# Gates and branch projections of a hybrid decoder layer as seven block products in two stages around attention

## The chip, the cores and the metric

One core of a Trainium2 chip runs the kernel. The metric is the device time of one execution in microseconds. Engines: TensorE (PE, matmuls; PEld is its weight load), VectorE (DVE), ScalarE (ACT), GpSimd (POOL), SyncE (SP, whose queue issues nearly all transfers).

## What is computed

One decoder layer over 1024 tokens of width 1024, float32. The reference, cut to what matters:

```
z = h @ w_in
hq, hf, hi, hg, sq, sk, sv, mq, gl = split_cols(z, IN_SPLITS)   # gl: 3 x 1024 gate columns
o_a = hgrn2(hq, hf, hi, lb)                    # 8 heads of 128, chunks of 64 tokens
o_a = rms_norm(o_a) * hg_norm_gain * silu(hg)
o_b = sliding_window_attention(sq, sk, sv, rel_bias, sinks)     # 16 heads, window 128
o_c = memory_attention(mq, mk, mv)             # 4 heads of 256, 256 memory tokens
gates = sigmoid(gl)
merged = (gates[0] * (o_a @ w_branch_hg) + gates[1] * (o_b @ w_branch_swa)
          + gates[2] * (o_c @ w_branch_mem))
h = layer_norm(alpha * h + merged @ w_out)
h = layer_norm(alpha * h + square(relu(h @ w_up)) @ w_down)
```

## The kernel before

**Products in three matmuls.** Every float32 operand is split in two parts: ACT casts it to the high part, DVE or POOL subtracts to get the low part (`split`, line 74). A product is then high times high, high times low and low times high. `zt` (line 99) makes 128 output columns for the 512 tokens of a half: 8 blocks of k, 24 matmuls of 512 columns. `weight` (line 78) loads 512 KB into a raw tile R, casts and subtracts into W; its subtraction goes to DVE every third time, else to POOL (line 70). There are four R and four W tiles, and the PSUM banks are three z, three s and two t.

**Stages.** First the keys and values of the memory tokens (lines 158 to 213). Then, for each half of the tokens (line 539): sliding-window attention (`swa_phase`), with gate blocks as matmul work between its units (`fill`); its eight branch projections (`proj`); memory attention by heads (`mem_head`); gates and projections in turn; HGRN2 (`hg_gates`, `hg_head`), where each head has a query product `z_q`, an output gate product `z_g`, a middle part `mid`, an output part `outp` and `last`; gates and projections again; then the product with w_out, LayerNorm and transposes (`flip_h1`, kept in `deferred`). Attention outputs stay on chip as split operands in O tiles; `merged` collects the gated sums. Weights of gates and projections are loaded and split once for each half.

**The up and down products** already use seven block products for two halves of the tokens and two halves of k (lines 700 to 952): of the eight products of half blocks one is saved, for sums and differences of the operands. `xs[1]` to `xs[7]` are the seven token operands, w1 to w4 the combined weights; a pair of weight blocks costs 7 x 12 = 84 matmuls. For the first 8 pairs (EARLY) two of the seven are made ahead by `first_two`.

**Order.** The code gives the tiles and a priority in program order; which instruction an engine takes next is then planned at build time by list scheduling on estimated durations, so that a weight of a later block may be cast before the result of an earlier one is read. Each engine and each queue then runs its list in order.

Of the kernel before, what the change touches and what calls it, by code (L numbers as in the profile page):

```python
# [15 lines left out]
P = 128  # L16
D = 1024
# [11 lines left out]
EARLY = 8  # L29

# [4 lines left out]
def hybrid_layer(ctx: ExitStack, tc: tile.TileContext, a: dict, out: bass.AP):  # L35
# [90 lines left out]
    bcon = st("MG", [P, 2048])[:32, :272]  # L126
# [3 lines left out]
    reset = const("reset", [P, 512])  # L130
    nc.vector.memset(reset, 1.0)
    nc.vector.memset(reset.rearrange("p (c t) -> p c t", t=64)[:, :, 0:1], 0.0)
    at = const("at", [P, 4, P])
    nc.gpsimd.memset(at, 0.0)
    state = const("state", [P, 8, P])
    carry = const("carry", [P, 3, P], F32R)
    vv = const("vv", [P, 5, P])
# [9 lines left out]
    d_h1t = dr.tile([P, NK, TH], F32, name="d_h1t")  # L147

    xsrc = a["xT"].rearrange("(k p) t -> p k t", p=P)
    msrc = a["memT"].rearrange("(k p) t -> p k t", p=P)  # L150
    mh = [st("T", [P, 4, MEM], F32R) for _ in range(2)]
    ml = [st("T", [P, 4, MEM], F32R) for _ in range(2)]
# [19 lines left out]
    x = (st("X", [P, NK, TH], F32R), st("X", [P, NK, TH], F32R))  # L172
    for h in range(4):
# [36 lines left out]
        if h < 3:  # L210
            load_x(xsrc[:, :, 0:TH], h, x, nc.vector)
            if h == 2:
                load_x(xsrc[:, :, 0:TH], 3, x, nc.vector)
# [13 lines left out]
    deferred = []  # L227

    def swa_unit(hf, tp, n, q, kk, bt, px, ob):
# [5 lines left out]
        def scores():  # L235
# [54 lines left out]
    def swa_phase(hf, x, merged, fill_last):  # L290
# [27 lines left out]
        def z_gate(m):  # L318
            o = zt(a["w_gate"][8 + m], *x)
            nc.scalar.activation(merged[m // 4][:, m % 4, :], o, AF.Tanh, scale=0.5)  # L320

# [7 lines left out]
        while deferred:  # L329
            deferred.pop(0)()  # L330
        oh = st("O", [P, NK, TH], F32R)
        ol = st("O", [P, NK, TH], F32R)
        pxa = st("T", [P, 2, 2, TH])
        pend = None
        for tp in range(4):
            if tp < 3:
                qn = st("T", [P, 2, 2, TH], F32R)
                fill = [lambda: z_sq(qn, tp + 1, 0), lambda: z_gate(2 * tp), lambda: z_sq(qn, tp + 1, 1),
                        lambda: z_gate(2 * tp + 1)]
            else:  # L340
                fill = [lambda: z_gate(6), lambda: z_gate(7)] + fill_last
            for n in range(4):
# [9 lines left out]
                def pend(pv=pv, n=n, tp=tp, ob=ob):  # L352
                    pv()
                    if n % 2:
                        cols = slice((n - 1) * P, (n + 1) * P)
                        src = ob.rearrange("p (n t q) -> p t n q", n=2, t=2)
                        for t in range(2):
                            evict_split(oh[:, 2 * tp + t, cols].rearrange("p (n q) -> p n q", n=2),
                                        ol[:, 2 * tp + t, cols].rearrange("p (n q) -> p n q", n=2), src[:, t])
            if tp < 3:  # L360
                q = qn
        pend()
        return oh, ol

    def gate(br, m, x):
        o = zt(a["w_gate"][8 * br + m], *x)
# [710 lines left out]
```

## Time and profile before

| | before |
|---|---|
| median of 3 runs | 2169.95 us (2169.92 to 2175.44) |
| the profiled execution | 2174.51 us, span 2171.3 us |
| PE busy, matmuls | 2096.4 us (97%), 10242 |
| DVE, ACT, POOL busy | 1141.3, 827.8, 844.8 us |
| HBM read, written | 216.78 MB, 44.58 MB |

Busy time of an engine counts the instructions that ran, also while they were held up; issue of transfers isn't counted. The span runs from the first to the last instruction of the profiled execution, whose own time is a little longer. What an engine's idle time costs is read from the stretch where it lies.

### The profile page before, as it was taken

To read this page: it belongs to the slowest core of one execution; us is meant where nothing else is said; L and a number is where in the kernel's file an instruction comes from. 1 tells how busy PE (TensorE), PEld (TensorE's weight loads), DVE (VectorE), ACT (ScalarE), POOL (GpSimd) and SP (SyncE) were. 2 spreads that over 40 slices of the span, in tenths; PEclk is the share of its full clock that TensorE was granted. 3 is DMA by queue.
4 is the path that set the end of the run, shared out by engine and by line. 5 is a ranking of instruction groups with operands and counts; after the bars stand their busy time and mean duration, and the time that the engine had idled before them with its cause. 6 is when DMAs were issued, how large, how long until landed. Compare 5 with 4: busy or idle time off the path is not lost.

```text
span 2171.3 us, 26697 instructions
## 1 busy us (share of the span) xinstructions
PE 2096.4 (97%) x10242; PEld 1725.8 (79%) x10242; DVE 1141.3 (53%) x2041; ACT 827.8 (38%) x1462; POOL 844.8 (39%) x401
## 2 busy tenths in 40 slices
PE   8999999999999999999999999996899998999987
PEld 8767888898988876678888898885788886888865
DVE  5566242244542366634315454137466565688888
ACT  5344242243433253424324343234444555433321
POOL 2212223423325441122343232554433435776675
PEclk9999999999999999999999999998899999999999
DMA  8411223222233541122332222344565446745322
GB/s 276 136 59 59 88 88 99 96 88 78 78 97 116 175 146 49 59 80 88 104 91 88 78 87 88 113 150 142 168 223 189 160 155 244 250 136 160 113 78 78
DMA packets 103422, 263.09 MB, mean 121 GB/s; under 512 B 9040, under 2 KB 22528, under 8 KB 103296
## 3 DMA queue, kind: packets, MB, share of 16 engines
q1 hardware_dynamic: 102400, 258.24, 36.7%
q10 hardware_dynamic: 896, 3.16, 0.4%
q8 instruction: 80, 1.31, 0.2%
q14 instruction: 46, 0.38, 0.1%
HBM read 216.78 MB, written 44.58 MB: 120 GB/s over the span
## 4 chain that ended last, share of the span: by engine, by line
PE 84%; DVE 5%; POOL 4%; issue 3%; DMA 2%; ACT 2%; SPq 0%; POOLq 0%; DVEq 0%; ACTq 0%
PE pz L60 59%; PE ps L60 17%; PE pt L60 7%; POOL W L76 1%; DMA R<-in_w_up_dram 1%; PE pt L274 1%; POOL sm L979 1%; DVE T L718 1%; ACT W L75 1%; POOL BT L76 0%; DVE R L718 0%; POOL O L994 0%; POOL MG L76 0%; DVE S L266 0%; DMA R<-d_ff 0%
## 5 line engine op out<-in xcount | busy, mean ns | idle before, releaser
L76 POOL TENSOR_TENSOR W<-R,W 128x1024 fp32r<-128x1024 f32 x200 | 485.9, 2430 | 1039.3 <-ACT W L75 1001.6
L60 PE MATMUL pz<-X,W 128*128 128x512 f32 x3360 | 821.8, 398 | 13.8 <-ACT W L75 10.1
L60 PEld LDWEIGHTS pz<-X,W 128*128 128x128 f32 x3360 | 628.5, 190 | 157.4 <-issue 11.5
L75 ACT CAST W<-R 128x1024 fp32r<-128x1024 f32 (+1 forms) x303 | 310.4, 1026 | 385.7 <-PE pz L60 156.0
L60 PE MATMUL pz<-O,W 128*128 128x512 f32 x1152 | 266.8, 390 | 0.0
L60 PEld LDWEIGHTS pz<-O,W 128*128 128x128 f32 x1152 | 215.8, 188 | 45.6 <-issue 0.8
L76 DVE TENSOR_TENSOR W<-R,W 128x1024 fp32r<-128x1024 f32 (+1 forms) x105 | 131.3, 1251 | 114.7 <-ACT W L75 114.3
L375 DVE SCALAR_TENSOR_TENSOR G<-G,pz 128x512 f32<-128x512 f32 x32 | 22.0, 687 | 174.1 <-PE pz L60 174.0
L60 PE MATMUL ps<-W,BT 128*128 128x512 f32 x360 | 98.9, 392 | 10.1 <-POOL BT L76 7.8
L60 PE MATMUL pz<-W,BT 128*128 128x512 f32 x354 | 97.4, 393 | 0.2 <-DVE X L880 0.2
L60 PE MATMUL pt<-O,W 128*128 128x512 f32 x384 | 93.9, 393 | 0.8 <-DVE T L718 0.8
L60 PE MATMUL pz<-W,X 128*128 128x256 f32 x768 | 93.7, 283 | 0.0
L60 PEld LDWEIGHTS pz<-W,X 128*128 128x128 f32 x768 | 92.9, 192 | 0.3
L76 POOL TENSOR_TENSOR BT<-R,BT 128x1024 fp32r<-128x1024 f32 x27 | 70.0, 2595 | 52.9 <-ACT BT L75 52.9
L60 PEld LDWEIGHTS ps<-W,BT 128*128 128x128 f32 x360 | 67.6, 188 | 25.8 <-POOL BT L76 8.2
L60 PEld LDWEIGHTS pt<-O,W 128*128 128x128 f32 x384 | 71.9, 189 | 18.5 <-DVE T L718 3.8
L76 POOL TENSOR_TENSOR MG<-R,MG 128x1024 fp32r<-128x1024 f32 (+1 forms) x30 | 78.9, 2632 | 16.5 <-ACT MG L75 16.5
L377 POOL TENSOR_TENSOR MG<-MG,G 128x512 f32<-128x512 f32 x32 | 42.3, 1321 | 99.7 <-DVE G L375 99.7
L60 PEld LDWEIGHTS pz<-W,BT 128*128 128x128 f32 x354 | 67.0, 190 | 15.4 <-DVE X L880 0.7
L60 PE MATMUL ps<-W,MG 128*128 128x512 f32 x252 | 68.2, 402 | 4.3 <-DVE O L880 4.3
L60 PE MATMUL ps<-W,T 128*128 128x256 f32 (+1 forms) x432 | 67.5, 294 | 0.0
L60 PE MATMUL pz<-W,MG 128*128 128x512 f32 x252 | 66.6, 396 | 0.0
(245 smaller groups left out, 3026.1 us busy)
## 6 DMA issues: line engine op xcount, KB each, us to landing
R<-d_ff SPq DMA_DIRECT2D x49, 512.0 KB, 3.6
R<-in_w_gate_dram SPq DMA_DIRECT2D x48, 512.0 KB, 3.5
R<-in_w_b_dram SPq DMA_DIRECT2D x48, 512.0 KB, 3.5
R<-in_w_up_dram SPq DMA_DIRECT2D x40, 512.0 KB, 4.2
d_ff<-T SPq DMA_DIRECT2D x58, 256.0 KB, 3.0
d_ff<-S SPq DMA_DIRECT2D x48, 256.0 KB, 2.5
T<-in_w_down_dram SPq DMA_DIRECT2D x12, 1024.0 KB, 5.5
R<-in_w_sq_dram SPq DMA_DIRECT2D x16, 512.0 KB, 3.6
```

The source lines that it names most:

```text
L60: nc.tensor.matmul(o, lhsT=l, rhs=r, start=start, stop=stop, skip_group_check=more)
L75: (hi_copy or nc.scalar.copy)(hi, src)
L76: (lo_eng or nc.gpsimd).tensor_tensor(out=lo, in0=src, in1=f32(hi), op=ALU.subtract)
L274: nc.tensor.transpose(o[:, c:c + P], pr[:, 2 * t + i, :], ident)
L375: nc.vector.scalar_tensor_tensor(out=t, in0=t, scalar=1.0, in1=o, op0=ALU.add, op1=ALU.mult)
L377: nc.gpsimd.tensor_tensor(out=mg, in0=mg, in1=th, op=ALU.add)
L718: nc.vector.tensor_tensor(out=o, in0=a_, in1=b_, op=op)
L979: nc.gpsimd.tensor_tensor(out=y, in0=e, in1=mhalf[:, :1], op=ALU.pow)
```

## The change

All gates (24 blocks of columns) and the HGRN2 output gate (8 blocks) are computed for both halves of the tokens in a stage of their own ahead of attention, as 16 pairs of blocks with seven products each; the results, after tanh (and for the output gate the product), go to DRAM (`d_z`). The left operand of x is split first, the other five are made from both halves (`combine`); four pairs make two of their products early (`two`). Attention then runs for both halves, one after the other. In it the forget gates `one` take the place of the gate blocks between the window units, `z_g` is gone (`zload` reads its result), the scalings of a unit's four rows are one instruction, and attention outputs are copied and stored in DRAM (`d_o`). During half 1 and the first projections, `job` loads the outputs of both halves, makes the combinations on POOL and stores them in `d_c`. A stage after attention then runs three branches in the order window, memory, HGRN2: seven operands loaded and split anew for each (`load_op`), two pairs early, four pairs of seven products, and `b_emit` multiplies by the gate loaded from `d_z` and adds to the merged sum, on POOL from the second branch on. Merged sums lie in `con`, T tiles and DRAM (`d_mg`) and are split by `merge_into`. Then the products with w_out run for both halves in a row, with half 0's transposes between half 1's blocks; the up stretch takes half 1's one at a time.

```diff
+    def combine(left, right, part, eng):
+        b11, b21, b12, b22 = left[0], left[1], right[0], right[1]
+        part(3, b22, 0)
+        eng.tensor_tensor(out=b11, in0=b12, in1=b11, op=ALU.subtract)
+        part(5, b11, 1)
...
+    def two(src, keep, emit):
+        w1 = halves(load_raw(src), nc.gpsimd)
+        o = pt("z")
+        prod(o, w1, 0, 1)
+        s1 = keep(o)
+        d = pt("s")
+        prod(d, w1, 1, 2)
+        emit(0, d, s1)
+
+    def seven(src0, src1, p1, emit):
+        r0 = load_raw(src0)
...
+        r1 = load_raw(src1)
+        add(r0[:, L], r0[:, L], r1[:, L], ALU.subtract)
+        add(r1[:, L], r1[:, L], r1[:, H])
+        w2 = halves(r1, nc.gpsimd)
+        add(r1[:, H], r1[:, H], r0[:, L], ALU.subtract)
+        w4 = st("W", [P, 2, 1024], F32R)
+        split(w4[:, 0, L], w4[:, 1, L], r1[:, H], nc.vector)
+        add(r0[:, H], r0[:, H], r1[:, H], ALU.subtract)
+        w3 = halves(r0, nc.gpsimd)
...
+        prod(o, w4, 0, 6, p1 is not None)
+        s2 = snap(o) if p1 is None else plus(o, p1)
+        b_ = pt("t")
+        prod(b_, w2, 0, 5)
+        prod(o, w3, 0, 7, False)
+        s3 = snap(o) if p1 is None else plus(o, p1)
+        emit(3, b_, s3)
+        c = pt("s")
+        prod(c, w2, 1, 4)
+        emit(1, c, s3)
+        prod(b_, w3, 1, 3, False)
+        emit(2, b_, s2)
...
+    for i in range(EARLY_Z):
+        two(zsrc(i)[0], z_keep(i), z_first(i))
+    for i in range(16):
+        seven(*zsrc(i), z_p1(i) if i < EARLY_Z else None, z_emit(i))
...
+    def job(br, k):
+        hs = (slice(0, TH), slice(TH, S))
+        t = []
+        for hv in hs:
+            raw = st("R", [P, 2, TH])
+            nc.sync.dma_start(raw, d_o[br, k:k + 5:4, :, hv].rearrange("k p t -> p k t"))
+            t.append((raw[:, 0], raw[:, 1]))
+
+        def part(j, src, e):
+            if j != 3:
+                nc.sync.dma_start(d_c[br, j - 4, k], src)
+
+        combine(t[0], t[1], part, nc.gpsimd)
...
-            for j in range(4):
-                nc.vector.tensor_scalar(out=pr[:, j, :], in0=pr[:, j, :], scalar1=dn[:, j:j + 1],
-                                        scalar2=None, op0=ALU.mult)
+            nc.vector.tensor_tensor(out=pr, in0=pr, in1=dn.unsqueeze(2).broadcast_to([P, 4, P]), op=ALU.mult)
...
+        for h in range(8):
...
+            if h < 7:
+                head(h + 1)
+            if h:
+                heads[h - 1][2]()
+            if h % 2 == 0 and h < 6:
+                g = h // 2 + 1
+                zv(vs[g // 2][:, g % 2], g)
+            heads[h][1]()
+            if h:
+                heads[h - 1][3]()
...
+            turn_b[0] += 1
+            split(xs[j][0][:, k:k + 2], xs[j][1][:, k:k + 2], raw, nc.gpsimd if turn_b[0] % 2 else nc.vector)
...
+        def emit(b, o, s_):
+            t = st("S", [P, 2, TH])
+            th, v = t[:, 0], t[:, 1]
+            nc.sync.dma_start(th, d_z[4 * br + i, b])
+            home = accs.get((i, b))
+            if home is None and e:
+                mg = st("G", [P, TH])
+                nc.sync.dma_start(mg, d_mg[slot[i, b]])
+            add(v, o, s_)
+            if e == 0:
+                dst = th if home is None else home
+                nc.vector.scalar_tensor_tensor(out=dst, in0=th, scalar=1.0, in1=v, op0=ALU.add, op1=ALU.mult)
+            else:
+                nc.vector.scalar_tensor_tensor(out=th, in0=th, scalar=1.0, in1=v, op0=ALU.add, op1=ALU.mult)
+                dst = th if home is None else home
+                nc.gpsimd.tensor_tensor(out=dst, in0=mg if home is None else home, in1=th, op=ALU.add)
...
+    for e in range(3):
+        br = order[e]
+        w = a[wname[br]]
+        for i in range(EARLY_B):
+            two(w[2 * i], lambda o, i=i: snap(o, p1s[i]), b_emit(e, i))
+            if i == 0:
+                operand_tiles()
+                load_op(br, 6)
+                load_op(br, 5)
+            else:
+                load_op(br, 7)
+                load_op(br, 4)
+                load_op(br, 3)
+        for i in range(4):
+            seven(w[2 * i], w[2 * i + 1], (lambda i=i: p1s[i]) if i < EARLY_B else None, b_emit(e, i))
+            if e == 0 and i in (1, 2):
+                job(0, i + 1)
+        if e < 2:
+            operand_left()
+            load_op(order[e + 1], 1)
+            load_op(order[e + 1], 2)
```

## Rows read from the trace of the kernel before

**Rows 1.** The page's first part: busy time, share of the span, instructions.

```profile
PE 2096.4 (97%) x10242; PEld 1725.8 (79%) x10242; DVE 1141.3 (53%) x2041; ACT 827.8 (38%) x1462; POOL 844.8 (39%) x401
```

**Rows 2.** The chain that ended last, shares of the span by engine.

```profile
PE 84%; DVE 5%; POOL 4%; issue 3%; DMA 2%; ACT 2%; SPq 0%; POOLq 0%; DVEq 0%; ACTq 0%
```

**Rows 3.** Busy time by stretch: length, engines (instructions), granted clock, DMA share, GB/s.

```profile
0.00:56.00 56.00, 49.27 (x387) 48.23 (x388) 30.92 (x43) 29.21 (x37) 12.74 (x10) 1.00 0.82 275
56.00:227.00 171.00, 167.16 (x805) 122.58 (x803) 105.60 (x366) 71.02 (x209) 34.24 (x16) 0.99 0.26 82
756.00:942.00 186.00, 175.70 (x850) 128.56 (x849) 124.03 (x389) 80.56 (x226) 48.70 (x26) 0.96 0.26 82
...
1700.00:1812.00 112.00, 112.00 (x494) 92.30 (x493) 62.51 (x75) 60.24 (x90) 43.23 (x18) 1.00 0.48 158
...
1850.00:2100.00 250.00, 249.73 (x1085) 203.59 (x1084) 201.76 (x216) 96.80 (x103) 180.38 (x69) 1.00 0.47 156
```

**Rows 4.** PE's instructions in order of time, projections and gates in turn (start, length).

```profile
342.71 5.60 PE L60 MATMUL pz<-O,W 128*128 128x512 f32 x24
348.15 5.60 PE L60 MATMUL pz<-X,W 128*128 128x512 f32 x24
```

**Rows 5.** The same view at the start of half 1; in brackets the idle time before.

```profile
776.04 1.11 PE L326 MATMUL pt<-cst,G 128*128 128x128 f32 x4 [3.84 <-ACT G L308]
776.80 8.11 PE L60 MATMUL pz<-X,W 128*128 128x512 f32 x24
784.76 1.04 PE L657 MATMUL pt<-cst,O 128*128 128x128 f32 x8
```

**Rows 6.** Groups by line and shape: busy us, mean ns of one, idle before.

```profile
L377 POOL TENSOR_TENSOR MG<-MG,G 128x512 f32<-128x512 f32 x32 | 42.3, 1321 | 99.7 <-DVE G L375 99.7
L76 DVE TENSOR_TENSOR W<-T,W 128x1024 fp32r<-128x1024 f32 x21 | 41.5, 1975 | 6.6 <-ACT W L75 6.5
...
L266 DVE TENSOR_SCALAR S<-S,sm 128x128 f32<-128x128 f32 x128 | 35.4, 340 | 0.6
...
L93 DVE TENSOR_TENSOR O<-ps,O 128x256 fp32r<-128x256 f32 x32 | 13.4, 419 | 11.6 <-ACT O L92 11.2
```

**Rows 7.** One line of the kernel: shortest, median and longest duration in ns.

```profile
L445 DVE TENSOR_SCALAR T<-T,c x16: 486/487/488, 419.7 to 1255.9; 128x512 f32<-128x512 f32 x16
```

**Rows 8.** Waits of PE: us in total, times, longest.

```profile
PE pt L274 <- DVE S L266: 10.1, 6, 1.9
```

**Rows 9.** One head: its stretch, then PE's and DVE's instructions in order.

```profile
607.67:622.95 15.28, 15.28 (x90) 13.27 (x88) 9.01 (x21) 5.99 (x15) 5.41 (x3) 1.00 0.22 70
...
614.12 0.83 PE L60 MATMUL ps<-BT 128*128 128x128 f32 x6
614.71 5.72 PE L60 MATMUL pz<-X,W 128*128 128x512 f32 x24
...
618.94 0.69 DVE L524 TENSOR_TENSOR BT<-ps,sm 128x512 f32<-128x512 f32 x1
```

**Rows 10.** POOL's and DVE's instructions in order of time, up and down products.

```profile
1706.22 2.41 POOL L76 TENSOR_TENSOR W<-R,W 128x1024 fp32r<-128x1024 f32 x1 [7.37 <-ACT W L75]
1708.94 2.51 POOL L76 TENSOR_TENSOR W<-R,W 128x1024 fp32r<-128x1024 f32 x1 [0.30 <-ACT W L75]
...
1707.38 1.81 DVE L718 TENSOR_TENSOR S<-T 128x512 f32<-128x512 f32 x1 [1.64 <-ACT T L727]
1709.11 0.68 DVE L718 TENSOR_TENSOR T<-ps,G 128x512 f32<-128x512 f32 x1
...
1711.92 0.68 DVE L718 TENSOR_TENSOR S<-T,S 128x512 f32<-128x512 f32 x1
...
1879.09 2.41 POOL L76 TENSOR_TENSOR BT<-R,BT 128x1024 fp32r<-128x1024 f32 x1 [2.68 <-ACT BT L75]
...
1880.34 2.23 DVE L76 TENSOR_TENSOR W<-T,W 128x1024 fp32r<-128x1024 f32 x1
```

**Rows 11.** The page's 40 slices: GB/s that the DMA engines moved.

```profile
GB/s 276 136 59 59 88 88 99 96 88 78 78 97 116 175 146 49 59 80 88 104 91 88 78 87 88 113 150 142 168 223 189 160 155 244 250 136 160 113 78 78
```

More of the change, by code (lines that the diff above doesn't have):

```diff
@@ L227, in hybrid_layer, with prod, snap @@
     deferred = []
+    L, H = slice(0, TH), slice(TH, 2 * TH)
+    def prod(o, w, g, j, start=True):
+        hi, lo = xs[j]
+        for k in range(4):
+            c = g * TH + k * P
+            wh, wl = w[:, 0, c:c + P], w[:, 1, c:c + P]
+            mm(o, wh, hi[:, k, :], start and k == 0, False, not start)
+            mm(o, wh, lo[:, k, :], False, False, not start)
+            mm(o, wl, hi[:, k, :], False, k == 3, not start)
+    def snap(o, t=None):
+        if t is None:
+            t = st("G", [P, TH])
+        nc.scalar.copy(t, o)
+        return t
@@ new lines, in add, with plus, load_raw, halves @@
+    def add(o, a_, b_, op=ALU.add):
+        nc.vector.tensor_tensor(out=o, in0=a_, in1=b_, op=op)
+    def plus(o, v):
+        t = st("G", [P, TH])
+        add(t, o, v)
+        return t
+    def load_raw(src):
+        t = st("R", [P, 1024])
+        nc.sync.dma_start(t, src)
+        return t
+    def halves(t, eng):
+        w = st("W", [P, 2, 1024], F32R)
+        split(w[:, 0, :], w[:, 1, :], t, eng)
+        return w
+    def two(src, keep, emit):
[6 more added lines that the diff above has]
+        emit(0, d, s1)
@@ L533, in last @@
                                            op1=ALU.mult)
-            split(oh[:, h, :], ol[:, h, :], sg, nc.vector)
-        return z_q, z_g, mid, outp, last
+            out_rows(0, h, 1, hf, sg.unsqueeze(1))
+        return z_q, mid, outp, last
     outv = out.rearrange("(b p) d -> b p d", p=P)
+    jobs = []
     for hf in range(NH):
-        merged = [st("MG", [P, 4, TH]) for _ in range(2)]
         q0 = []
@@ new lines, in hybrid_layer, with load_op @@
+        if hf == 0:
+            x = nx
+        heads[7][2]()
+        heads[7][3]()
+    order = (1, 2, 0)
+    wname = ("w_b0", "w_b1", "w_b2")
+    turn_b = [0]
+    def load_op(br, j):
+        for k in range(0, 4, 2):
+            if j > 3:
+                src = d_c[br, j - 4, k:k + 2]
+            else:
+                src = d_o[br, k + (4 if j > 1 else 0):k + (6 if j > 1 else 2), :, slice(TH, S) if j == 3 else slice(0, TH)]
+            raw = st("R", [P, 2, TH])
+            nc.sync.dma_start(raw, src.rearrange("k p t -> p k t"))
+            turn_b[0] += 1
+            split(xs[j][0][:, k:k + 2], xs[j][1][:, k:k + 2], raw, nc.gpsimd if turn_b[0] % 2 else nc.vector)
```

400 lines of the change are left out of this document (227 added, 173 removed).

## The prediction

> **What bounds the kernel now.** I read the shares of the engines first: TensorE (PE) is busy 97% of the span, ScalarE (ACT), VectorE (DVE) and GpSimd (POOL) 38 to 53% [rows 1]. Then the chain of work that ended last: 84% of it is PE [rows 2]. Then busy time by stretch [rows 3]: in the squared-ReLU up stretch PE is busy 112.00 of 112 us, so there a matmul less is time less; the start of the second token half (756 to 942) has 10.3 us of idle PE and a granted clock of 0.96, the same work of the first half (56 to 227) 3.8 us and 0.99. So the time is PE's count of columns, plus what its transitions lose. The change is worth what it takes off PE, as long as the other engines keep up in the two new stages; that has to be read stage by stage.
>
> **1. Matmuls removed.** Before: 24 column blocks of gates, 8 of the HGRN2 output gate and 24 of branch projections, each in two token halves of 24 matmuls: 2688. After: 28 pairs of blocks, 7 products of 12: 2352 (the early `two` calls only move two of the seven). 336 fewer. Consecutive blocks of 24 start 5.44 us apart [rows 4], 0.2267 us each: **-76.2 us**. The count is fixed by the code; that the products are not fewer is no rival.
>
> **2. The turn from half 0 to half 1.** W_out, its LayerNorm and the start of sliding-window (SWA) work of half 1 no longer meet. The two SWA stretches differ by 15 us (186 against 171) [rows 3]; a 3.84 us wait and then 24 matmuls at 8.11 us instead of 5.44 show where [rows 5]. Some 4.1 us of it are 32 transposes (1.04 us per 8), which move to the W_out loop: **-11 us** (-15 to 0). Half 0's LayerNorm now lies beside half 1's W_out, 43.5 us of matmuls (8 blocks of 24): hidden; what may be late there is the splitting of merged tiles, +3 (0 to 10). Half 1's LayerNorm ends as before, ahead of the up stretch: 0 (-4 to +4).
>
> **3. SWA units.** Four DVE scalings per unit (0.340 us each, 128 in all) become one op over 512 (taken as 0.69), the split of outputs on DVE (13.4 us in all) goes; two 0.49-us ops per HGRN2 gate come in from a stretch where DVE had time. PE waited 10.1 us for those scalings, six times [rows 6 to 8]: **-4 us** (-10 to +2).
>
> **4. The operands of x.** For the seven products each of four k pairs now costs DVE seven more 512-element ops (0.68 us), 19 us in all, and 2 MB more are loaded. The memory stage has DVE busy 30.9 of 56 us, ACT 29.2, DMA at 0.82 of its engines [rows 3]. The right half is hidden by the four early `two` calls (4 x 5.44 = 21.8 us of PE) that need the left one alone: **+4 us** (0 to +20, if the raw buffers, four and now held by longer chains, starve the weights).
>
> **5. Stage Z (gates, 16 calls of `seven`).** Its nearest rows are the up loop: per pair 19.1 us of PE, no idle, POOL 43 and DVE 62.5 of 112 us [rows 3]. `seven` is the same but for holding the last product over to the next pair; the accumulation into `b_` then waits for an ACT copy and a DVE add under one product (2.72 us): **+5 us** (0 to 16, 1 us a call), and +2 into attention. Writing and reading 16.8 MB of gates lies beside it.
>
> **6. Attention without its filler.** Between a head's products `z_g` (5.44 us) goes. Before, an HGRN2 head without `v` has a period of 15.28 us with DVE busy 9.01; its output is normalised at 619.6, 4.9 us after the PE part ended at 614.7 [rows 9], and `z_g` covered it. After, only `mid` (2.4 us) is sure to stand there, unless the next query product is drawn forward. 10 of the 16 heads have no `v` product beside them; 0 to 2.5 us each, I take 1: **+10 us** (0 to 25). DVE falls to some 7.6 of 9.8 us: it fits. The `job` subtractions (1.32 us each on POOL [rows 6]) stand in one queue with the small power that this chain needs; that is in the 10.
>
> **7. The branch stage, where the forecast is decided.** POOL and DVE there exclude each other, as the up loop shows [rows 10]: POOL runs 1706.22 to 1708.63; the DVE add of two SBUF tiles that starts at 1707.38 ends at 1709.19, 0.56 us after POOL, and takes 1.81 us instead of 0.68. The add that reads PSUM (1709.11) keeps 0.68 under the next POOL op. The same with 1024 elements: a DVE split started at 1880.34 ends 1.07 us after POOL's end at 1881.50. So one resource serves POOL ops and DVE ops with two SBUF inputs, and their pure times add up: POOL 2.40 us per 1024 [rows 10], 1.32 per 512 [rows 6], DVE 1.07 and 0.55. The Trainium skill, "SBUF — State Buffer", section "Who interferes with whom", states this as a rule: a VectorE op with two SBUF inputs and a GpSimd op that reads SBUF wait for one another for the whole instruction. By that rule the sum below holds; without it only the engines' own sums count, and the term would be near 25; the trace agrees, by the 0.56 and 1.07 us.
> Over the three branches: POOL 36 weight splits and 21 of the 42 operand splits at 2.40 (136.8), 32 merging adds, 8 `job` subtractions and 8 splits of merged tiles at 1.32 (63.4): 200.2 us. DVE: 48 weight subtractions, 12 half splits, 48 gate products and 8 splits at 0.55 (63.8), 21 operand splits at 1.07 (22.5): 86.3. Sum 286.5. Ahead of the stage can lie the first two operands and two weights (11.7), behind it six splits (5.6): 269 us. PE needs 3 x 76.2 = 228.5. In the second and third branch alone it is some 94 us against 76.2. The stretch 1850 to 2100 shows the other side [rows 3]: 69 POOL ops, 166 us of the resource, 21 DVE splits of 1.07, 22 us [rows 6], and about as many sums, in 250 us, and PE busy 249.73. Under its limit it costs nothing; over it, the excess shows: 269 - 228.5 = 40.5, and 10 for idle time of the resource where operand buffers come free late (at the start and at two changes of branch): **+51 us** (+15, if the excess is partly drawn into attention, to +89, with the second rival's 38 on top). The reload at a change, 7 MB of operands and some 4 MB of weights and gates in 36 us, would be 305 GB/s where the best slice shows 276 [rows 11]; it lies under the same stretch and adds nothing as long as that is stretched. SP's queue takes some 280 more stores and loads; the loads of gates stand behind stores of results in it, which is in this term too.
>
> **Sum**: -76.2 - 11 + 3 - 4 + 4 + 5 + 2 + 10 + 51 = -16.2 us. The profiled execution takes 2174.51 us, 3.2 around its span of 2171.3, so 2158.3; the median of the runs, 2169.95, is 4.6 below it: **2154 us**. Own range 2138 to 2172: term 7 off by a third, 17 us, either way.
>
> **Rivals.**
> *The excess is hidden* (2128): if POOL's backlog is worked off under heads and W_out, or the planner draws `two` calls of the branch stage into the heads' gaps, term 7 is 25. That is the bare changes: at one, POOL alone has 7 operand splits, 4 weight splits and 6 adds, 34 us, in the 30 us of products from the moment X is free; with late buffers 8 us, three times. For: `two` needs only X, free since half 0. Against: 94 against 76 us recurs in branches two and three, with nothing else to run.
> *The merging adds hold PE up* (slower, 2192): each of 48 output blocks takes one of two S buffers from the load of its gate to the end of its add on POOL, and 32 have that add. If a weight split of 2.40 us stands before the add, both S are held, the PSUM block isn't emptied and PE stops. Half of the 32 give 38 us over the sum. It decides from 9 blocks on: 22 us, and the kernel is slower than before. For: POOL is the fullest engine there, and in order. Against: three z and three s banks give a product or two of slack, and part of this wait is the excess already counted.
> *The heads keep their period* (slower, some 2231): if 15.28 us is latency and not PE's sum, removing `z_g` frees nothing: 16 x 5.44 = 87 instead of 10. Against: DVE is busy only 9.01 of 15.28, and PE 15.28.
>
> **How the numbers follow.** Chances: forecast 0.42, excess hidden 0.22, adds hold PE up 0.18, heads 0.08, a mixture of smaller ones 0.10, half on each side. A difference under 0.3% (6.5 us: 2163.4 to 2176.5) can't be told from none here. Of the forecast's 0.42 some 0.29 lie under 2163.4, 0.10 within, 0.03 above. Faster 0.29 + 0.22 + 0.05 = 0.56, same 0.10, slower 0.03 + 0.18 + 0.08 + 0.05 = 0.34. The range has to hold the hidden excess and the adds: 2115 to 2205, with the heads' case and the tails left out.
>
> **What would show it.** Right: PE count 9906, no idle in stage Z, a branch stage of some 280 us with PE busy about 80%, POOL busy nearly throughout, DVE ops of two SBUF tiles at 1 to 3 us there and 0.68 elsewhere. Wrong at step 7: a branch stage under 250 us with POOL waiting; wrong at 6: heads at 15 us; wrong at 4: PE idle before 80 us. The prediction falls if the loss sits outside the branch stage, or if there is none.

## The result and the profile after

The changed kernel takes 2313.45 us (median of 4 runs, 2307.84 to 2317.01) against 2171.0 us for the kernel before on the same chip (4 runs, 2169.92 to 2175.44): the ratio is 1.065, with an interval of 1.0623 to 1.0676. It is 6.5% slower; the prediction of 2154 us, a gain of 0.7%, was wrong in sign and by 159 us.

The first part of the page of the changed kernel, to be read beside [rows 1]: busy time, share of the span, instructions.

```profile
PE 2066.2 (90%) x9906; PEld 1681.6 (73%) x9906; DVE 1375.7 (60%) x2173; ACT 895.2 (39%) x1556; POOL 1002.9 (43%) x479
```

The 336 matmuls are gone, as step 1 counted them. But PE's busy time fell by 30.2 us and not by 76: part of what is left ran at a lower clock. And PE now stands idle for some 240 us of 2306, where it stood for 75. So the question is in which stretch it stands.

The changed kernel by stage: length, PE, PEld, DVE, ACT and POOL busy (instructions), granted clock, share of the DMA engines, GB/s. The stages are the memory keys, the gates (Z), attention of half 0 and of half 1, the branches, W_out.

```profile
0.00:71.00 71.00, 55.35 (x387) 53.05 (x388) 48.98 (x63) 37.24 (x52) 20.20 (x15) 0.93 0.67 234
71.00:390.00 319.00, 312.22 (x1347) 252.83 (x1347) 133.13 (x175) 121.38 (x172) 121.60 (x52) 0.99 0.40 128
390.00:751.00 361.00, 342.64 (x1921) 279.92 (x1920) 212.24 (x498) 153.34 (x375) 83.13 (x40) 0.99 0.31 98
751.00:1169.00 418.00, 367.92 (x2086) 299.78 (x2085) 245.26 (x564) 151.89 (x402) 137.55 (x81) 0.96 0.37 126
1169.00:1510.00 341.00, 256.29 (x1014) 201.08 (x1015) 184.56 (x193) 108.83 (x127) 201.43 (x98) 0.87 0.54 179
1510.00:1611.00 101.00, 94.29 (x417) 77.17 (x417) 49.74 (x72) 31.73 (x39) 55.00 (x31) 0.97 0.56 200
```

The first row answers to the first of [rows 3]: the same 387 matmuls in 71 us instead of 56. The two attention rows have the same work; half 1 takes 57 us more, with POOL busy 137.55 instead of 83.13. The branch row is the worst: 1008 matmuls at 0.2267 us are 228.5 us; the stage takes 341, of which PE is busy 256.29 (so 28 us more than at full clock, the granted clock is 0.87) and idle 85.

Before, the work of these stages lay mixed. To compare, products of 24 matmuls are taken out of the halves at 5.44 us each [rows 4]: half 0 of before took 656.4 us with 56 such blocks, half 1 673.8 with 56, W_out 43.5 a half.

| stage | before, us | after, us | difference | predicted |
|---|---|---|---|---|
| memory keys, x | 56 | 71 | +15 | +4 |
| Z (64 blocks of before) | 348.2 | 319 | -29 | -36.5 |
| attention, both halves | 351.7 + 369.1 | 361 + 419 | +59 | -5 |
| branches (48 blocks) | 261.1 | 340 | +79 | +18 |
| W_out, both halves | 87 | 101 | +14 | +3 |
| rest | 698 | 695 | -3 | 0 |
| sum | 2171 | 2306 | +135 | -16 |

(Predicted: Z is -43.5 of matmuls, +5, +2; attention -11, -4, +10, where the -11 has already taken off 4 us of transposes that go to W_out; branches -32.7 of matmuls, +51.)

Two places in the trace show what happens. First half 1 of attention, in order of time (start, length, engine, line; in brackets the idle time before and what ended it): POOL, then DVE, then PE.

```profile
1058.81 1.26 POOL L198 TENSOR_TENSOR R<-R,R 128x512 f32<-128x512 f32 x1 [5.47 <-DMA R<-d_o]
1060.15 1.26 POOL L200 TENSOR_TENSOR R<-R 128x512 f32<-128x512 f32 x1
1061.49 1.26 POOL L202 TENSOR_TENSOR R<-R,R 128x512 f32<-128x512 f32 x1
1062.83 1.26 POOL L204 TENSOR_TENSOR R<-R,R 128x512 f32<-128x512 f32 x1
1064.05 1.01 POOL L1187 TENSOR_TENSOR sm<-sm,mhalf 128x4 f32<-128x4 f32 x1
...
1065.09 0.16 DVE L1188 TENSOR_TENSOR sm<-sm 128x4 f32<-128x4 f32 x1 [11.73 <-POOL sm L1187]
...
1067.12 1.12 PE L702 MATMUL pt<-cst,S 128*128 128x128 f32 x4 [13.48 <-DVE S L696]
```

POOL waits in order for a job's load (L198), makes its four subtractions, and only then the power of 4 elements (L1187) that the head's norm needs. DVE waits 11.73 us for it, PE 13.48.

Second, the change from the first projected branch to the second: SP's issues, ACT, PE.

```profile
1303.89 0.92 SPq L799 DMA_DIRECT2D R<-d_o  x2
1306.27 3.85 SPq L304 DMA_DIRECT2D R<-in_w_b_dram  x2
1310.18 0.90 SPq L832 DMA_DIRECT2D S<-d_z  x2
1313.26 17.75 SPq L304 DMA_DIRECT2D R<-in_w_b_dram  x5
...
1311.09 1.04 ACT L77 CAST O<-R 128x1024 fp32r<-128x1024 f32 x1 [0.28 <-DMA R<-d_o]
1315.72 1.04 ACT L77 CAST W<-R 128x1024 fp32r<-128x1024 f32 x1 [3.59 <-DVE R L295]
...
1299.10 2.88 PE L62 MATMUL ps<-X,W 128*128 128x512 f32 x12
1316.82 1.22 PE L62 MATMUL pt<-O,W 128*128 128x512 f32 x2 [14.83 <-ACT W L77]
1319.25 1.65 PE L62 MATMUL pt<-O,W 128*128 128x512 f32 x3 [1.21 <-POOL W L78]
1320.70 4.75 PE L62 MATMUL pz<-MG,W 128*128 128x512 f32 x12
```

The weights of the first `seven` are issued behind the operand loads, at 1306.27; the pair is combined on DVE, cast on ACT at 1315.72, and PE has waited 14.83 us. The twelve matmuls that start at 1320.70 take 4.75 us instead of 2.88: from 1316.8 to 1326 us the granted clock is 0.58 of full speed, so after the idle time it is mostly at the lower of its two levels, which adds to the loss. The largest waits of PE over the whole branch stage (total us, times, longest) are:

```profile
PE pt L62 <- ACT W L77: 40.9, 3, 14.8
PE pz L62 <- ACT W L77: 16.7, 3, 9.8
PE pt L62 <- DVE S L295: 11.0, 6, 4.3
```

Six waits for freshly cast weights are 57.6 us; the largest three are the first `seven` of each branch.

### The profile page after: what moved, and what is told of

Its sections match the earlier page's. It is cut to its first block, busy times and chain, and to the rows that moved or that the text cites. A ratio compares the mean times of both kernels' runs of the same rounds, so it can differ in the third digit from the quotient of the medians.

```text
span 2306.0 us, 27081 instructions
## 1 busy us (share of the span) xinstructions
PE 2066.2 (90%) x9906; PEld 1681.6 (73%) x9906; DVE 1375.7 (60%) x2173; ACT 895.2 (39%) x1556; POOL 1002.9 (43%) x479
## 5 line engine op out<-in xcount | busy, mean ns | idle before, releaser
L62 PE MATMUL pz<-X,W 128*128 128x512 f32 x1344 | 344.8, 406 | 30.9 <-ACT W L77 20.8
L62 PEld LDWEIGHTS pz<-X,W 128*128 128x128 f32 x1344 | 254.2, 194 | 95.9 <-ACT W L77 22.4
L62 PE MATMUL pt<-O,W 128*128 128x512 f32 x1056 | 265.4, 400 | 58.0 <-ACT W L77 40.9
L62 PEld LDWEIGHTS pt<-O,W 128*128 128x128 f32 x1056 | 198.5, 191 | 112.6 <-ACT W L77 42.2
L62 PE MATMUL pz<-BT,W 128*128 128x512 f32 x528 | 132.2, 400 | 16.2 <-DVE G L295 14.8
L62 PE MATMUL pz<-MG,W 128*128 128x512 f32 x528 | 134.2, 402 | 0.0
L62 PE MATMUL ps<-X,W 128*128 128x512 f32 x528 | 129.4, 394 | 0.0
L62 PE MATMUL ps<-T,W 128*128 128x512 f32 x528 | 127.2, 389 | 0.0
L62 PEld LDWEIGHTS pz<-MG,W 128*128 128x128 f32 x528 | 103.1, 196 | 23.3 <-ACT W L77 0.9
L62 PEld LDWEIGHTS ps<-X,W 128*128 128x128 f32 x528 | 101.1, 191 | 21.6
```

The source lines that it names most:

```text
L62: nc.tensor.matmul(o, lhsT=l, rhs=r, start=start, stop=stop, skip_group_check=more)
```

## The experiments

Each kernel was run once, beside a run of the kernel before on the same chip (2168.4 to 2176.4 us); the changed kernel is at 2308 to 2317, median 2313.45, from which differences are taken unless another kernel is named. A few microseconds between two runs are not read as a difference. "Stage" times are read from the start and end of PE's groups in each trace.

**Weights first at a change of branch.** The first `seven` of a branch is cut in two: loading and splitting (`prep`) goes ahead of the five operand loads, the products stay.

```diff
-                load_op(br, 6)
-                load_op(br, 5)
...
+        first = prep(w[0], w[1], lambda: p1s[0], b_emit(e, 0))
+        operand_tiles()
+        for j in (6, 5, 7, 4, 3):
+            load_op(br, j)
```

> In each branch the weights of the first call of seven are loaded and combined ahead of the operand loads 6, 5, 7, 4 and 3, which all follow the second call of two. Theory A (the weights stand behind ten operand loads in the four raw buffers and in SP's queue): the three waits for a cast weight before the first seven, 12.3, 14.8 and 13.8 us, go; some of it comes back as waits for operands, so the branch stage falls from 341 to 290 to 320 us, and the kernel by 20 to 50 us. Theory B (POOL and DVE exclude each other and the stage is full by that): the same work in another order, branch stage 335 to 345 us.

2307.81 us, no difference; theory A is out, and the stage, at 333 us, is near theory B's 335 to 345, which the experiments on POOL's load below test by themselves. PE's three waits for these weights fell from 40.9 to 11.2 us in all, and others took their place: 10.2 us for low halves of an operand on POOL, and smaller ones. The order decides which part of the reload PE waits for, and hardly how long.

**The 32 merging adds left out.**

```diff
-                dst = th if home is None else home
-                nc.gpsimd.tensor_tensor(out=dst, in0=mg if home is None else home, in1=th, op=ALU.add)
+                dst = mg if home is None else home
```

> The 32 additions to the merged sums on POOL (second and third branch) are left out. Theory B (shared resource of POOL and DVE is the bound): 32 x 1.32 = 42 us less there, so 30 to 42 us off the branch stage of 341. Theory A (order of loads): only waits behind those additions go, 17.7 us of waits of PE for S and G tiles at most: 5 to 20 us off, and the waits for a cast weight at the three branch starts stay at 12 to 15 us.

2298.12 us, theory A; the stage falls from 340 to 327, POOL's busy time there from 201 to 166 us. The adds cost 12 us, not the 38 of the rival that they hold PE up.

**The jobs left out:** loads, subtractions and stores.

```diff
-                job(1, h)
...
-                    job(2, h - 1)
...
-                src = d_c[br, j - 4, k:k + 2]
+                src = d_o[br, k:k + 2, :, slice(0, TH)]
```

> The 12 jobs (loads, subtractions on POOL and stores of the combined attention outputs) are left out; operands 4 to 7 are loaded from plain outputs instead. Theory C (the subtractions wait on POOL for their loads, and the small power of the HGRN2 chain stands behind them): attention of half 1 falls from 418 to 360 to 375 us, the level of half 0 (361). Rival (the second half is slower because the output gate product is gone from its heads): it stays above 405, as half 0 would then be slow too. Branch stage: up to 10 us less.

2267.26 us: 41 to 50 us less than the four runs of the changed kernel. The same three stretches of half 1, first the changed kernel, then this one:

```profile
902.00:992.00 90.00, 83.87 (x436) 66.00 (x434) 55.94 (x112) 40.39 (x97) 40.83 (x24) 1.00 0.55 184
992.00:1052.00 60.00, 57.50 (x373) 52.03 (x374) 36.53 (x47) 28.98 (x52) 26.91 (x15) 0.97 0.49 167
1052.00:1112.00 60.00, 45.30 (x300) 40.97 (x299) 23.33 (x56) 14.59 (x41) 24.77 (x17) 0.89 0.43 150
```

```profile
902.00:992.00 90.00, 85.82 (x449) 68.05 (x448) 50.93 (x116) 40.65 (x97) 19.21 (x8) 1.00 0.26 86
992.00:1052.00 60.00, 55.89 (x373) 50.35 (x371) 35.98 (x49) 28.87 (x51) 15.85 (x7) 1.00 0.38 128
1052.00:1112.00 60.00, 54.30 (x365) 49.41 (x364) 28.33 (x64) 22.49 (x49) 19.64 (x10) 0.94 0.34 112
```

65 matmuls more fit into the last stretch. Attention of half 1 isn't 360 to 375 us as expected: it is 382 to the first product of the branch stage, which comes at 1134.4 instead of 1179.8 us and mixes with the last heads, and 408 to its own last transposes. So theory C holds for a part, and half 1 stays longer than half 0 without any job.

**x: the combinations moved out of the memory stage,** with a second load of the left half, under the four early `two` calls of stage Z.

```diff
-        x_right(h, x_left(h))
+        x_left(h)
...
         two(zsrc(i)[0], z_keep(i), z_first(i))
+        again = st("R", [P, 2, TH])
+        nc.sync.dma_start(again, xsrc[:, i:i + 5:4, 0:TH])
+        x_right(i, again)
```

> The combinations of x for the right operands are made under the four early calls of two, from a second load of the left half, and no longer in the memory stage. If the memory stage is long (71 us for 56) because of raw buffers and DVE work of these combinations: it ends at 56 to 60, stage Z takes 319 to 325, 8 to 15 us less in all. If it is the additional bytes and the Z stage then waits for operands: no more than 3 us less.

2318.0 us, a miss. The memory stage is back at 56.3 us (-15), and stage Z takes 334.2 (+15). The combinations cost some 15 us at either place: four `two` calls don't cover them. That their own weights go through the same queues may be why; no run shows it.

**Operands kept** from the first branch.

```diff
+            if e:
+                continue
             if i == 0:
                 operand_tiles()
                 load_op(br, 6)
...
-        if e < 2:
-            operand_left()
-            load_op(order[e + 1], 1)
-            load_op(order[e + 1], 2)
```

> Left out: the operands of the second and the third projected branch are not loaded again; their products use those of the first. Theory A (the loss in the branch stage is the reload at each change of branch: loads, casts and low halves in front of the products): the stage, 340 us in the changed kernel from the last transposes of attention to the first product of W_out, falls by 45 to 80 us, and the run is at 2235 to 2270 us. Theory B (the loss is the chain of combinations, casts and low halves inside each seven-product round, with the merging adds, which all stay): it falls by 20 us at most, and the run is above 2293 us.

2267.82 us, at the edge of theory A: 41 us of the stage (340 to 299) go with the two reloads. By step 7's prices the 28 splits that are gone would also free its shared resource by 14 x (2.40 + 1.07) = 49 us, so this run alone doesn't tell step 7 from theory A; the adds above and the low halves below do. What is left, in this run by stretch:

```profile
1171.00:1250.00 79.00, 44.12 (x159) 33.45 (x160) 37.30 (x38) 23.56 (x25) 46.70 (x22) 0.76 0.62 209
1250.00:1323.00 73.00, 68.98 (x294) 55.88 (x293) 38.21 (x49) 18.07 (x22) 29.13 (x14) 0.97 0.45 153
1323.00:1396.00 73.00, 64.98 (x276) 52.32 (x275) 38.27 (x45) 16.67 (x21) 42.44 (x24) 0.98 0.43 142
1396.00:1469.00 73.00, 65.89 (x284) 52.62 (x284) 44.29 (x48) 22.16 (x32) 44.80 (x25) 1.00 0.37 115
```

In the first 79 us there are 159 matmuls where 348 would fit at 0.2267 us: 43 us are lost in and about the first start. In the other 219 us there are 854 where 966 would fit: 25 us are lost in steady rounds. So the 112 us are 43 + 41 + 25, and a small rest.

**Branches as plain products.** Gates stay in seven products; the branches, still from DRAM in their own stage, use `zt` for one half and then the other, and the operands of the next half (two X or two O tiles) load meanwhile. No jobs.

```diff
+        for m in range(8):
+            plain(e, m, 0, w, xl)
+            if e == 0 and 0 < m < 5:
+                load_half(br, m - 1, 1, xr)
...
+        for m in range(8):
+            plain(e, m, 1, w, xr)
+            if e < 2 and 1 < m < 6:
+                load_half(order[e + 1], m - 2, 0, xl)
```

> Gates and output gates stay as seven products in their own stage; the branch projections, still in their own stage and from DRAM, are eight plain products again, half by half, the other half's operands loading meanwhile; no jobs. 144 matmuls more at 0.2267 us are 32.7 us; the jobs gave back 40 in their own run. Theory A (what the branch stage loses comes with the seven-product form, that is from seven operands to reload with no second buffer): the excess of 112 us over the products falls to 10 to 40, and the run is at 2200 to 2245 us. Theory B (it comes from what stays, the merging adds and the way through DRAM): the excess stays above 80 and the run is at 2275 us or more. At or under 2171 neither holds.

2206.11 us, theory A: 107 us less than the changed kernel with 144 matmuls more. Its branch stage:

```profile
1170.00:1230.00 60.00, 60.00 (x267) 49.67 (x266) 17.74 (x19) 15.39 (x15) 19.14 (x8) 1.00 0.62 210
1230.00:1290.00 60.00, 60.00 (x267) 49.67 (x266) 22.98 (x21) 18.00 (x18) 29.37 (x16) 1.00 0.71 230
1290.00:1350.00 60.00, 60.00 (x266) 49.71 (x265) 24.99 (x21) 16.57 (x17) 32.73 (x19) 1.00 0.68 230
1350.00:1405.00 55.00, 55.00 (x244) 45.53 (x244) 17.64 (x17) 14.70 (x18) 37.73 (x23) 1.00 0.47 151
```

PE is busy throughout, at the full clock, with the same merging adds, the same way through DRAM and, on average, more GB/s (207) than the 179 of the changed kernel. What the stage lost came with the seven-product form. Which part of that form it was, this run doesn't say: it changes several things at once (no jobs, no combined weights, 24 operand splits instead of 42 and all on DVE, a second set of tiles, the first operands loaded under the last heads). The kernel is still slower than the one before beside it (2176.41).

**Jobs: loads at the start of the slot, subtractions at its end.**

```diff
+            jl = job_load(1, h) if hf else None
             sc()
-            if hf:
-                job(1, h)
...
             rest()
+            if hf:
+                job_run(1, h, jl)
```

> Nothing left out: in attention of half 1 each job's two loads are issued at the start of its slot and its five subtractions at the slot's end, instead of both at one place. Theory A (the jobs cost because GpSimd stands still at its first subtraction until the load lands, up to 12.5 us, and the head's small power queues behind): 20 to 37 us of the 40 come back, 2273 to 2293 us. Theory B (the cost is the subtractions themselves and the traffic): under 10 us come back, 2303 us or more.

2324.75 us, slower. (A job has four subtractions, not the five of this expectation.) Less comes back than nothing, so theory A's 20 to 37 us don't show: half 1 takes 427 us instead of 419, and PE's longest wait for a head's norm is 15.5 us instead of 13.5. Two of the four R buffers are now held for a whole slot, which may be the cause, so that theory A isn't tested by this kernel; two with buffers of their own, below, are.

**Low halves of operands on DVE.**

```diff
-            split(..., raw, nc.gpsimd if turn_b[0] % 2 else nc.vector)
+            split(..., raw, nc.vector)
```

> Nothing left out: the low halves of all branch operands are made on VectorE, 21 of them taken from GpSimd (2.4 us each there, 1.2 here). Theory A (the reload's order and latency, not GpSimd's filling): within 8 us of the changed kernel, 2305 to 2321 us. Theory B (GpSimd is nearly full in this stage, as the prediction had it): 15 to 40 us less, 2273 to 2298 us.

2309.25 us, theory A, no difference: POOL's busy time in the stage falls from 201 to 151 us, and the stage still takes 340.

**Jobs in the X buffers, at their old place; then with early loads too.**

```diff
+            ring_t[:] = [st("X", [P, NK, TH]) for _ in range(2)]
+        ring.append(n)
+        return ring_t[n // 4][:, 2 * (n % 4):2 * (n % 4) + 2, :]
...
-            raw = st("R", [P, 2, TH])
+            raw = job_raw() if len(ring) < 20 else st("R", [P, 2, TH])
```

> Nothing left out: the ten jobs of attention in half 1 load into the X buffers, which lie idle then, instead of two of the four R buffers; they stand where they stood. Theory A (the jobs cost because they hold R buffers, so that weights come late; the kernel with early loads held them longer and lost 11 us): 15 to 35 us of the 40 come back, 2278 to 2298 us. Theory B (they cost because GpSimd waits in order for the landing): within 6 us of the changed kernel.

> Nothing left out: jobs in the X buffers, and their loads issued a slot ahead of the subtractions. Theory A (R buffers): as the run with the X buffers alone, within 6 us. Theory B (GpSimd's wait in order): 20 to 35 us under the changed kernel, 2278 to 2293 us, where the X buffers alone gave nothing. If both are needed each alone gives little and the two together 20 or more. If it stays above 2303 us, it is the subtractions themselves on GpSimd (50 in attention at 1.29 us) or their traffic.

2309.8 and 2303.52 us: 4 and 10 us less. The buffers aren't it. The first time lies within theory B's 6 us, but with the loads early as well theory B asks for 2278 to 2293 us, so the wait for the landing isn't it either. What holds, by half a microsecond, is the last line of the second expectation: the subtractions or their traffic. The long wait of PE for a head's norm fell from 13.5 to 6.2 us in both, so the stall shown above was real, but it was a small part of the 40. (40 subtractions in attention, not 50.)

**Gate loads of the branch stage from POOL's queue.**

```diff
-            nc.sync.dma_start(th, d_z[4 * br + i, b])
+            nc.gpsimd.dma_start(th, d_z[4 * br + i, b])
```

> Nothing left out: in the branch stage the 48 loads of gates are issued from GpSimd's queue instead of SyncE's. Theory A (SyncE stands in order at these loads until a merging add on GpSimd frees the S buffer, 57.7 us in all where it was read, and the weights of the next round queue behind): 15 to 40 us less, 2273 to 2298 us. Theory B (those stands of SyncE lie beside the longer chain of loads, casts and low halves): within 8 us of the changed kernel, or slower.

2326.33 us, theory B, slower. Each issue takes 0.56 us of POOL (median of 48), which had to make the low halves.

**Everything in plain products,** gates too: the new arrangement with the 10242 matmuls of the kernel before.

```diff
+    for m in range(32):
+        w = z_weight(m)
+        if m >= 4:
+            z_plain(m, 0, w)
+        z_plain(m, 1, w)
```

> Nothing left out: as the kernel with plain branch products (2206 us), and the stage of gates ahead of attention in plain products too, one load of a weight for both halves, without the combinations of x. 192 matmuls more at 0.2267 us are 43.5 us. Theory A (the stage's own losses, 15 us in the memory stage and 14 in the stage of gates, come with the seven-product form): 15 to 29 of it come back, 2220 to 2235 us. Theory B (those losses come from the way through DRAM and the start of the stage): under 5 come back, 2245 us or more.

2219.19 us, at the edge of theory A: 13 us more than with the gates in seven products (21 where each is taken against the kernel before beside it), instead of 43.5. Its memory stage ends at 56.3 us; then stage Z and attention of half 0:

```profile
56.00:404.00 348.00, 348.00 (x1539) 288.22 (x1538) 31.49 (x32) 74.76 (x103) 58.74 (x25) 1.00 0.34 116
404.00:764.00 360.00, 341.10 (x1920) 278.72 (x1919) 209.67 (x495) 152.62 (x371) 82.56 (x40) 0.99 0.30 96
```

The arrangement alone, with no product saved, is 51 us slower than the kernel before (2168.42): attention of half 0 by 8 us, that of half 1 by some 28, W_out by 13.

**The four jobs of the last branch moved into the rounds of the first; then the first left operands loaded at heads 4 to 7.**

```diff
-            if e == 0 and i in (1, 2):
-                job(0, i + 1)
+            if e == 0:
+                job(0, i)
...
+                if h > 3:
+                    load_op(1, 1 + (h - 4) // 2, (2 * (h % 2),))
```

> Nothing left out: as the kernel with jobs in the X buffers and loads a slot ahead (2303.5 us), and the four jobs of branch 0, which is projected last, all stand in the four rounds of the first projected branch; none is left at heads 6 and 7. Theory A (the larger part of the jobs' 40 us is that the two jobs at heads 6 and 7 stand in order ahead of the first operand loads of the branch stage): the products of the stage begin before the last transposes of attention, as in the run without jobs, and the run is at 2270 to 2288 us. Theory B (the cost is the subtractions and their traffic wherever they stand): above 2297 us.

> Nothing left out: as the kernel before it in this list, and the left operands of the first branch are loaded piece by piece at heads 4 to 7. Theory A (the start of the branch stage loses some 40 us because its loads begin when attention ends): 8 to 25 us under that kernel. Theory B (the start is set by the seven-product rounds and the five other operands, which still load there): within 5 us of it.

2300.61 and 2298.40 us. The branch products do begin before the last transposes, at 1140.7 us in the first, but the time isn't given back: theory B both times. The place of these jobs isn't the cost, and an early left operand alone doesn't help.

**Only the stores of the jobs left out (first line of the edit); then all kept, but the stores a slot later.**

```diff
-                nc.sync.dma_start(d_c[br, j - 4, k], src)
...
+                later.append(lambda: nc.sync.dma_start(d_c[br, j - 4, k], src))
...
+                flush()
                 job_run(1, h, jl)
```

> Left out: only the 48 stores of the jobs' combinations; loads, places and all subtractions of the jobs stay as in the changed kernel, and the branch stage loads four tiles that are ready in place of the combinations. Theory A (SyncE issues in order, and each job's four stores stand there waiting for GpSimd's subtractions while the loads of weights and operands queue behind): 20 to 40 us less, 2273 to 2293 us, near the run without jobs (2267). Theory B (the cost is the subtractions on GpSimd and what they hold up there): under 10 us less, 2303 us or more.

> Nothing left out: as the kernel with jobs in the X buffers and loads a slot ahead (2303.5 us), and the four stores of each of the ten jobs in attention are issued one slot later, when their subtractions are done. Theory A (SyncE waits at these stores): 8 to 25 us under it, 2278 to 2296 us. Theory B (the subtractions on GpSimd): within 5 us of it.

2310.05 and 2302.87 us: theory B both times. SP does wait at these stores, and no time shows for it.

**Only the 48 subtractions left out; then all kept, and the subtractions on DVE** (the last line of the edit).

```diff
-        combine(t[0], t[1], part, nc.gpsimd)
+        for j, src in ((5, t[0][0]), (7, t[1][0]), (6, t[1][1]), (4, t[0][1])):
+            part(j, src, 0)
...
+        combine(t[0], t[1], part, nc.vector)
```

> Left out: only the 48 subtractions of the twelve jobs on GpSimd (four each, 1.29 us: 62 us of GpSimd; the expectations before this one counted five); their loads stay, and their stores store what was loaded. Theory A (of the three parts of a job it is the subtractions, since neither stores nor buffers nor the loads' place mattered): 25 to 40 us less, 2273 to 2288 us, as without jobs. Theory B (loads and stores together are the cost, each alone being hidden by the other): under 12 us less, 2300 us or more.

> Nothing left out: as the kernel with X buffers, early loads and late stores (2302.9 us), and the 48 subtractions are made by VectorE (0.68 us each, 33 us) instead of GpSimd (62 us). Theory A (what GpSimd's in-order queue holds up, the small powers of the heads and the low halves of weights, is the cost): 10 to 30 us under it, 2273 to 2293 us. Theory B (VectorE is on the heads' chain itself, and waits there in order as GpSimd did): within 6 us of it or slower.

2281.41 and 2290.90 us: theory A. The subtractions are 32 of the jobs' 46 us (from the median; 26 of 41 from the fastest run of the changed kernel), and 12 come back when DVE makes them (from 2302.87). The stretches of half 1 without them, where the loads and stores still run (0.54 and 0.62 of the DMA engines):

```profile
902.00:992.00 90.00, 86.78 (x450) 68.58 (x449) 49.75 (x120) 40.56 (x101) 17.03 (x8) 1.00 0.54 179
992.00:1052.00 60.00, 54.91 (x362) 49.36 (x361) 37.68 (x46) 29.74 (x46) 17.01 (x7) 1.00 0.62 206
1052.00:1112.00 60.00, 58.03 (x419) 53.67 (x419) 27.85 (x70) 18.13 (x54) 13.57 (x8) 1.00 0.35 119
```

## Why the prediction was wrong

The 142 us between the two times come apart by the runs, to within a few: the new arrangement costs some 51 (everything plain), the gates in seven products give back 13 to 21, the branches in seven products cost 107, of which 41 to 50 go with the jobs. For the first the sum had -2 (steps 2, 3, 6 and W_out), for the second a gain of 32, for the last a loss of 18.

*Step 1* was right: 9906 matmuls. In the middle of stage Z (191 to 311 us) PE is busy 120.00 of 120 us, so `seven` at its steady rate costs nothing, as step 5 took it from the up loop.

*Step 7 failed,* and with it the forecast. It said that POOL and DVE share a resource whose 269 us exceed PE's 228.5, so that the stage would be stretched evenly to some 280 us with "POOL busy nearly throughout", and that the reload at a change "adds nothing as long as that is stretched". The exclusion is there, as in [rows 10]: in the changed kernel's branch stage the DVE product of two SBUF tiles that starts under a POOL operation takes 2.23 us and ends 0.55 us after it, while a sum that reads PSUM takes 0.68:

```profile
1299.38 2.23 DVE L842 SCALAR_TENSOR_TENSOR S<-S 128x512 f32<-128x512 f32 x1 [1.58 <-DMA S<-d_z]
...
1303.97 0.68 DVE L295 TENSOR_TENSOR S<-ps,con 128x512 f32<-128x512 f32 x1
...
1298.67 2.39 POOL L78 TENSOR_TENSOR BT<-R,BT 128x1024 fp32r<-128x1024 f32 x1 [2.02 <-ACT BT L77]
```

So the exclusion holds. (The trace agrees with the rule of the Trainium skill, "SBUF — State Buffer", "Who interferes with whom", that the two wait for one another.) The work was summed about right too: added up from the trace, POOL's operations and DVE's with two SBUF inputs, overlaps counted once, fill 277 of the stage's 340 us. But the resource didn't set the time: it is free for 63 us where the step gave 10. With low halves on DVE it would be relieved by 21 x (2.40 - 1.07) = 28 us (it is then filled for 255), and the stage stayed at 340; without the adds by 42 (filled for 244), and it fell by 12. POOL was busy 201 of 341 us. The time goes where the step gave 10 us: 43 at the first start and 41 with the two reloads, where seven operands in single buffers have to be loaded, cast and subtracted while the weights of the first rounds go through the same four R tiles and the same in-order queues. Four rounds later the same begins again. Which link of this reload holds PE up longest stays open. The order of the loads, low halves on DVE and an early left operand changed little; more raw tiles or second operand buffers for the seven products, and fewer bytes, were not tried. Bytes are a rival at the first change, where from 1305 to 1316 us, with PE idle, the DMA engines are busy 0.94 of the time at 336 GB/s; in the wait at the second, 1420 to 1432, it is 0.68 at 249. The 25 us of the steady rounds stay open as well. In stage Z the same operands serve sixteen rounds, and the up loop has as many: that row [rows 3] was the nearest, but it holds no change of operand. The step's "+89" end of the range was closer than its value; the measured term is +112.

*Step 6* had the place of its worst part in one sentence and sized it at nothing: the subtractions of the jobs in one queue with the small power "that is in the 10". Attention without its filler is +9 us in half 0 alone, about all that the step gave both halves; half 1 is +50, of which some 25 are the subtractions (419 us against 394 without them). How these 25 are shared between the in-order wait and the exclusion with DVE isn't settled: both are there. The exclusion reaches the small steps of the norm on DVE, which take about 0.16 us elsewhere. In the last head three of them run beside a job's last subtractions and a split, and each ends 0.02 or 0.03 us after POOL's operation; PE then waits 8.30 us (DVE, then POOL):

```profile
1163.15 1.22 DVE L1188 TENSOR_TENSOR sm<-sm 128x4 f32<-128x4 f32 x1 [1.12 <-POOL sm L1187]
1164.60 1.12 DVE L1190 TENSOR_SCALAR sm<-sm 128x4 f32<-128x4 f32 x1
1165.76 2.25 DVE L1191 TENSOR_TENSOR sm<-sm,sm 128x4 f32<-128x4 f32 x1
...
1163.08 1.26 POOL L202 TENSOR_TENSOR R<-R,R 128x512 f32<-128x512 f32 x1
1164.43 1.27 POOL L204 TENSOR_TENSOR R<-R,R 128x512 f32<-128x512 f32 x1
1165.66 2.33 POOL L78 TENSOR_TENSOR X<-R,X 128x1024 fp32r<-128x1024 f32 x1
```

The run with the subtractions on DVE returned some 12. Another part of half 1's excess is the end of attention, which has no products of gates and projections to run beside the last heads; everything plain has 28 us there without any job.

*Step 2* took -11 us for the turn between the halves and didn't get it. Without W_out beside it, window attention of half 1 is still the longer one: from the first transposes at its start (779.5 us) to its last it takes 161 us against 151 in half 0; before it was 162 against 150. So in the changed kernel W_out isn't the reason of that difference; what is stays open. *Step 4* was mis-sized: +15 instead of +4. It said that the right half is hidden by four `two` calls; the run that put the combinations there lost the same 15 in stage Z. *Step 5* had +7 and measured +14, some 8 of it in the ramp behind the memory stage, where from 71 to 131 us 227 matmuls stand for 264 that would fit. *W_out* is +14 against +3: 4 of it are transposes that step 2 moved there, 6.7 are two waits of PE at the turn of its halves.

*The rivals.* Merging adds that hold PE up would have been 38 us over the sum; the adds cost 12 of the stage, so this isn't it. The heads that keep their period would have shown in half 0 and didn't. The hidden excess is refuted. That the reload itself, and not the filling of an engine, holds PE up stood in no rival.

No kernel of this study is faster than the one before. The best of the new arrangement is gates in seven products and plain branches, 30 us slower.

## What to carry to other kernels

A product form that needs more operands is worth its saving only where the operands stay for many rounds: sixteen rounds without a change still gave back only 13 to 21 of the 43.5 us saved, their start taking the rest, and four rounds with a reload lost more (112 us) than a branch stage of plain, double-buffered products had to pay (33 us). The sum of a resource's load gives no more than a lower bound for a stage: here it came out as summed (277 us by the trace against 269) and the stage took 340. So work out the changes of operands one by one too: what is free at that moment, and through how many single buffers, queues and bytes the first product's inputs come. And subtractions that are put on an engine because it is half idle are not free if that engine also has one small step of a serial chain, or holds up the engine that has the others.

## What the runs showed of the hardware that was not expected

A transfer issued by GpSimd took 0.56 us of that engine (48 of them), against 0.32 us on SyncE's queue, and the run was slower. A DVE operation with a single SBUF input can wait for POOL too, which step 7's rule left out: the 128x4 scaling at L1190 took 1.12 us beside a POOL subtraction, with which it ended, and 0.17 in the median of 16. After an idle time of 14.83 us twelve of PE's matmuls took 4.75 us instead of 2.88 at a granted clock of 0.58, so mostly at the lower of its two levels (1.2 against 2.4 GHz); over the branch stage, where the granted clock is 0.87, PE is busy 28 us longer than its matmuls take at 0.2267 us each, beside the 85 us of idle time.
